# Fetching the down weights of one FFN pair ahead of the next pair's gate and up products

## The chip, the cores and the metric

The kernel runs on one core of one Trainium2 chip. The metric is the time of one execution on the device, in microseconds (us); lower is better. TensorE (PE in the profile) does the matrix products, VectorE (DVE) and ScalarE (ACT) the elementwise work, GpSimd (POOL) some subtractions, and SyncE (SP) issues every DMA of this kernel from a single queue.

## The reference

One layer on a sequence of 2048 tokens with 1024 features. After an RMS norm the input is projected; stick-breaking attention (4 heads), chunked softmax attention with a relative bias (8 heads) and a short gated convolution run side by side; their normalised outputs go through one output projection and are added to the input. Then comes the feed-forward network (FFN), with 2816 hidden features:

```python
def stick_breaking_attention(q, k, v):      # 4 heads of 64
    for o in range(n):                      # key block i - o for query block i, 128 x 128
        z = jnp.einsum('bhnqd,bhnkd->bhnqk', qb[:, :, o:], kb[:, :, :n - o])
        log_rest = jax.nn.log_sigmoid(-z)   # masked on the diagonal
        after = jnp.einsum('bhnqj,js->bhnqs', log_rest, after_mat) + carry[:, :, o:, :, None]
        w = jnp.exp(jax.nn.log_sigmoid(z) + after)
        out = out.at[:, :, o:].add(jnp.einsum('bhnqk,bhnkd->bhnqd', w, vb[:, :, :n - o]))
        carry = carry.at[:, :, o:].add(jnp.sum(log_rest, axis=-1))

def swiglu(x, w_gate, w_up, w_down):
    return (jax.nn.silu(x @ w_gate) * (x @ w_up)) @ w_down

        x = x + y @ w_out[l]
        x = x + swiglu(rmsnorm(x, ffn_norm_w[l]), w_gate[l], w_up[l], w_down[l])
```

## The kernel before

**Two halves, woven.** The 2048 tokens are worked on in two halves of two groups of 512 tokens. `weave()` writes TensorE's program: it alternates pieces of attention with steps of a generator `fill()`, which holds the projections and then, for the first half's two groups, the output projection and the FFN (`ffn_group`). So the FFN of the first half runs beside the attention of the second half. TensorE's order is fixed by the order in which the code is written. The other engines and the SP queue are put in order by a scheduler, and each then runs its own list in order: an instruction that waits holds everything behind it on that engine.

**An attention piece** of the stick-breaking heads computes scores on TensorE (L583 to L586, into one of three `sc` buffers), two sigmoids on ScalarE (L605 and L606, which read the `sc` buffer and so free it), a running product over the keys on VectorE (the scan at L609), a product (L614), transposes on TensorE (L548), their copy to 16 bits (L550 on ScalarE, L551 on VectorE), and the product with the values (L561, L566).

**The FFN of a group.** The 2816 hidden columns are cut into 22 blocks of 128. `gated(f)` makes one block: 24 products for the gate and 24 for the up projection (L318 to L320; each 32-bit operand is held as two 16-bit parts), then tanh and products (L851 to L854), and its high and low parts `gh` (L856) and `gl` (L857). Blocks go in pairs. The product with the down weights of a pair, `down(prev)`, comes after the first block of the next pair: for each of 8 tiles of the output, 6 products into an `sc` buffer (L868 high weight, L869 low weight, L870 high weight with `gl`) and an addition to the row on VectorE (L871). `down` is called for a "set" of two blocks of weights, eleven times a group.

**The weights.** `load_down(f)` brings one block of down weights: a DMA of 512 KB into a raw buffer `wr` (L254), a cast to the high part `wh` on ScalarE (L256), and a subtraction for the low part `wl` on GpSimd (L258). The gate and up weights come through `Weights`: `load` fetches two raw blocks (L179) and sums their squares on ScalarE (L181) to find a scale, and `split` scales and casts them on ScalarE (L223, L224), subtracts on GpSimd (L225) and stores the parts to DRAM (L229). This is done while the first group runs; the second group reloads the parts. `get(f)`, at the start of `gated(f)`, also calls `split` for block f+1 and `load` for block f+2. All raw weights, of the gate, up and down projections, share **one ring of four `wr` buffers**: a load must wait until the buffer's last reader, a GpSimd subtraction (L225 or L258), is done. All split parts share a ring of eight.

Of the kernel before, what the change touches and what calls it, by code (L numbers as in the profile page):

```python
# [34 lines left out]
def f32(ap):  # L35
    return ap.bitcast(F32)
# [3 lines left out]
def trunk(ctx: ExitStack, tc: tile.TileContext, x, anw, w_in, qnw, knw, biasx, conv_w, onw, w_out,  # L40
          fnw, w_gate, w_up, w_down, out):

    nc = tc.nc
# [44 lines left out]
    def sc1():  # L88
        return ps.tile([128, 512], F32, name="sc", tag="sc", bufs=3)
# [161 lines left out]
    def load_down(f, low):  # L251

        raw = wp.tile([128, D], F32, name="wr", tag="wr", bufs=4)
        nc.sync.dma_start(raw, w_down[f * 128:(f + 1) * 128, :])  # L254
        hi = wp.tile([128, D], F32R, name="wh", tag="w16")
        nc.scalar.copy(hi, raw)  # L256
        lo = wp.tile([128, D], F32R, name="wl", tag="w16")
        low.tensor_tensor(lo, raw, f32(hi), ALU.subtract)  # L258
        return hi, lo
# [462 lines left out]
    def y_norms(half):  # L722
        assert traced[half], half
        groups = HALVES[half]
        gain = gain_row("o")
        for i, g in enumerate(groups):
            for t in range(4):
                later(6.0 * (4 * i + t), lambda T=g * 4 + t: y_norm(T, gain))
# [47 lines left out]
    def fill():  # L776

        H = [{}, {}, {}]
        W = stream
        rows = [x_rows(H[0], HALVES[0]), x_rows(H[1], HALVES[1]), y_rows(H[2], HALVES[0])]  # L780
        for half, groups in enumerate(HALVES):
            if half == 0:
                yield from rows[0].ahead()
                rows[0].patient = True
            yield from v_block(H[half], groups, W, C_VA, 0, rows[half])
            if half == 0:
                late_consts()
            yield from stick_qk(H[half], groups, W, 0)
            later(8.0, lambda half=half: done.add((half, 0)))
            yield from stick_qk(H[half], groups, W, 1)  # L790
            later(8.0, lambda half=half: done.add((half, 1)))
            yield from conv_block(H[half], groups, W, 0)
            for p in range(4):
                if half == 1 and p == 3:
                    y_norms(0)
                if p % 2 == 0:
                    yield from v_block(H[half], groups, W, C_VB + 128 * p, 4 + 2 * p)
                yield from chunk_qk(H[half], groups, W, p)
                later(20.0, lambda p=p, half=half: done.add((half, 2 + p)))
            yield from conv_block(H[half], groups, W, 1, rows[half + 1].ahead)  # L800
        yield from out_proj(H[2], HALVES[0], W, rows[2], frows[0])
        for g in HALVES[0]:
            yield from ffn_group(g, frows[0], g == HALVES[0][-1])
# [9 lines left out]
    def paired(f):  # L813

        if f not in PAIRED:
            ds = DS["gu", f][0]
            e = consts.tile([128, 2], F32, name=f"gu{f}")
            nc.vector.tensor_scalar(e[:, 0:1], ds[:, 0:1], 0.5, None, op0=ALU.mult)
            nc.vector.tensor_tensor(e[:, 1:2], e[:, 0:1], ds[:, 1:2], ALU.mult)
            PAIRED[f] = e  # L820
        return PAIRED[f]

    def hidden(u, h):

        (wh, wl), (hh, hl) = u, h
        o = acc()
        yield from mm3(o, lambda k: wh[:, k, :], lambda k: wl[:, k, :], lambda k: hh[:, k, :],
                       lambda k: hl[:, k, :], KT)
        return o

    def ffn_group(g, rows, last):

        yield from rows.need(g, 2)
        h = rows.H[g]
        X1 = []
        with tc.issue_after(last_row[0].ins):
            for t in range(4):
                x1 = xp.tile([128, D], F32, name="x1", tag="xt")
                nc.sync.dma_start(x1, x1d[g * 4 + t])
                X1.append(x1)  # L840

        def part(name):
            return ap.tile([128, 520], F32R, name=name, tag="w2")[:, :GRP]

        def gated(f):

            u = stream.get(("gu", f))
            e = paired(f)
            o = yield from hidden(u[0], h)
            sg = ap.tile([128, 520], F32, name="sg", tag="w2")[:, :GRP]  # L850
            nc.scalar.activation(sg, o, AF.Tanh, scale=e[:, 0:1])  # L851
            nc.vector.scalar_tensor_tensor(sg, sg, 1.0, o, op0=ALU.add, op1=ALU.mult)  # L852
            o = yield from hidden(u[1], h)
            nc.vector.scalar_tensor_tensor(sg, sg, e[:, 1:2], o, op0=ALU.mult, op1=ALU.mult)  # L854
            gh, gl = part("gh"), part("gl")
            nc.scalar.copy(gh, sg)  # L856
            nc.vector.tensor_tensor(gl, sg, f32(gh), ALU.subtract)  # L857
            return gh, gl

        def down(G, W):  # L860
            n = len(G)
            for t in range(4):
                cs = slice(t * 128, (t + 1) * 128)
                for c in range(2):
                    cc = slice(c * 512, (c + 1) * 512)
                    o = sc1()
                    for i, ((gh, gl), (wh, wl)) in enumerate(zip(G, W)):
                        nc.tensor.matmul(o, gh[:, cs], wh[:, cc], start=i == 0, stop=False)  # L868
                        nc.tensor.matmul(o, gh[:, cs], wl[:, cc], start=False, stop=False)  # L869
                        nc.tensor.matmul(o, gl[:, cs], wh[:, cc], start=False, stop=i == n - 1)  # L870
                    nc.vector.tensor_tensor(X1[t][:, cc], o, X1[t][:, cc], ALU.add)  # L871
                    yield 0.65 * n

        prev = None
        for i in range(0, NF, 2):
            G = []
            for f in range(i, min(i + 2, NF)):
                G.append((yield from gated(f)))
                if prev is not None:
                    yield from down(prev[0], [load_down(e, nc.gpsimd) for e in prev[1]])  # L880
                    prev = None
            prev = (G, range(i, i + len(G)))
            if i in (8, 14):
                if last:
                    if i == 14:
                        y_norms(1)
                else:
                    yield from rows.ahead()
        yield from down(prev[0], [load_down(e, nc.gpsimd) for e in prev[1]])
        for t in range(4):  # L890
            T = g * 4 + t
            nc.sync.dma_start(out[T * 128:(T + 1) * 128, :], X1[t])
# [197 lines left out]
```

## Time and profile before

| | |
|---|---|
| time, median of 3 runs | 2824.76 us (2823.86 to 2832.62) |
| profiled execution | 2830.86 us, of it 2829.0 us from first to last instruction |
| mean granted TensorE clock | 0.958 of full speed |
| busy: TensorE, VectorE, ScalarE, GpSimd | 2590.3, 1567.4, 1067.8, 465.3 us |
| TensorE's share of the span | 92% |
| `wr` loads of down weights (L254) | 66 of 512 KB, median 4.1 us from issue to landing |

The profile is of one execution. The engines run side by side, so their busy times don't add up to the span. The idle time of an engine is put down to the instruction or DMA that ended last before it went on ("x waited for y"). Idle time matters where the engine is the one that the others wait for.

### The profile page before, as it was taken

What the parts mean: (1) busy time and instruction counts of PE and PEld (TensorE: products, weight loads), DVE (VectorE), ACT (ScalarE), POOL (GpSimd) and SP (SyncE); (2) the same over time, 40 slices, a digit from 0 to 9 for tenths busy, and PEclk for the clock granted to TensorE, in tenths of its full rate; (3) what the DMA queues carried; (4) which work ended last, traced back from release to release, by engine and by line L of the source; (5) the groups of instructions that cost most, each with busy time, mean ns of one, the idle gap of its engine ahead of it and who ended that gap; (6) DMA issues with size and microseconds to landing.
All of it is one profiled execution on the core that took longest, in us unless ns stands there. A gap on an engine that the chain in (4) does not pass through costs nothing. (4 is left out here: it accounts for less than half of the span.)

```text
span 2829.0 us, 41973 instructions
## 1 busy us (share of the span) xinstructions
PE 2590.3 (92%) x16258; PEld 1742.9 (62%) x16258; DVE 1567.4 (55%) x3601; ACT 1067.8 (38%) x2016; POOL 465.3 (16%) x433
## 2 busy tenths in 40 slices
PE   5998899999879888887889999997999999999999
PEld 4476667688557645554556666653774555665556
DVE  5456876556986665666666666645333223333224
ACT  5465555444444554554554444421112111111110
POOL 1123310022321122223222111123000000000000
PEclk8999999999989988998899999998999999999999
DMA  7544465454348543243336444234563111111101
GB/s 240 181 154 138 124 200 155 145 149 154 127 166 259 162 124 110 93 129 127 105 117 203 144 133 139 92 133 165 197 195 122 53 45 60 45 45 61 51 23 60
DMA packets 254567, 362.42 MB, mean 128 GB/s; under 512 B 78240, under 2 KB 169376, under 8 KB 254368
## 3 DMA queue, kind: packets, MB, share of 16 engines
q1 hardware_dynamic: 254368, 359.75, 39.8%
q8 instruction: 127, 2.08, 0.3%
q14 instruction: 72, 0.59, 0.1%
HBM read 254.81 MB, written 104.86 MB: 127 GB/s over the span
## 5 line engine op out<-in xcount | busy, mean ns | idle before, releaser
L318 PE MATMUL acc<-hh,w 128*128 128x512 f16 x1728 | 661.4, 383 | 13.8 <-DVE sg L852 11.0
L319 PE MATMUL acc<-hl,w 128*128 128x512 f16 x1728 | 658.8, 381 | 0.0
L320 PE MATMUL acc<-hh,w 128*128 128x512 f16 x1728 | 658.4, 381 | 0.0
L318 PE MATMUL acc<-w,hh 128*128 128x256 f16 x1408 | 393.8, 280 | 4.0 <-ACT w L224 4.0
L319 PE MATMUL acc<-w,hh 128*128 128x256 f16 x1408 | 392.3, 279 | 1.8 <-POOL w L225 1.8
L320 PE MATMUL acc<-w,hl 128*128 128x256 f16 x1408 | 392.2, 279 | 0.1
L320 PEld LDWEIGHTS <-w 128*128 128x128 f16 x1728 | 170.0, 98 | 207.0 <-issue 5.9
L318 PEld LDWEIGHTS <-w 128*128 128x128 f16 x1728 | 169.9, 98 | 178.8 <-issue 21.5
L319 PEld LDWEIGHTS <-w 128*128 128x128 f16 x1728 | 170.3, 99 | 166.4 <-issue 17.5
L551 DVE SCALAR_TENSOR_TENSOR wtl<-tp,wth 128x512 f16<-128x512 f32 (+3 forms) x384 | 197.3, 533 | 133.4 <-ACT wth L550 133.2
L609 DVE TENSOR_TENSOR_SCAN re<-re,zero 128x512 f32<-128x512 f32 (+3 forms) x160 | 221.7, 1386 | 73.2 <-ACT re L606 72.7
L225 POOL TENSOR_TENSOR w<-wr,w 128x1024 f16<-128x1024 f32 x76 | 165.6, 2199 | 452.8 <-ACT w L224 283.9
L997 DVE SCALAR_TENSOR_TENSOR sg<-acc,ds,sg 128x512 f32<-128x512 f32 x44 | 33.0, 751 | 346.8 <-PE acc L320 346.8
L868 PE MATMUL sc<-wh,gh 128*128 128x512 f32 x352 | 161.2, 458 | 60.8 <-ACT wh L256 50.7
L550 ACT ACTIVATE wth<-tp 128x512 f16<-128x512 f32 (+3 forms) x384 | 171.8, 471 | 96.0 <-PE tp L548 92.7
L574 POOL TENSOR_TENSOR yu<-yu 128x64 f32<-128x64 f32 x192 | 75.0, 391 | 723.1 <-ACT yu L573 696.6
L1019 DVE TENSOR_TENSOR x<-sc,x 128x512 f32<-128x512 f32 x176 | 121.6, 692 | 109.6 <-PE sc L1017 109.0
L869 PE MATMUL sc<-wl,gh 128*128 128x512 f32 x352 | 151.2, 429 | 25.5 <-POOL wl L258 25.5
L871 DVE TENSOR_TENSOR x<-sc,x 128x512 f32<-128x512 f32 x176 | 120.6, 688 | 92.4 <-PE sc L870 90.0
L652 ACT ACTIVATE s<-s,nm 128x640 f32<-128x640 f32 (+4 forms) x128 | 97.4, 761 | 182.0 <-DVE nm L650 181.7
L583 PE MATMUL sc<-k,q 128*128 128x320 f32 (+3 forms) x384 | 164.6, 433 | 1.3 <-DVE hl L276 1.3
L256 ACT CAST wh<-wr 128x1024 fp32r<-128x1024 f32 x66 | 68.6, 1042 | 246.4 <-PE sc L1016 180.1
(168 smaller groups left out, 4614.7 us busy)
## 6 DMA issues: line engine op xcount, KB each, us to landing
w<-wd SPq DMA_DIRECT2D x136, 512.0 KB, 4.1
wd<-w SPq DMA_DIRECT2D x76, 512.0 KB, 2.7
wr<-in_w_down SPq DMA_DIRECT2D x66, 512.0 KB, 4.1
q<-qd SPq DMA_DIRECT2D x192, 128.0 KB, 2.9
k<-kd SPq DMA_DIRECT2D x56, 256.0 KB, 3.9
wr<-in_w_gate SPq DMA_DIRECT2D x22, 512.0 KB, 4.2
wr<-in_w_up SPq DMA_DIRECT2D x22, 512.0 KB, 5.7
xt<-in_x SPq DMA_DIRECT2D x16, 512.0 KB, 5.0
```

Of the source, the lines that this page charges most:

```text
L225: nc.gpsimd.tensor_tensor(w[:, 1, :], raw, w[:, 0, :], ALU.subtract)
L318: nc.tensor.matmul(o, sh(k), mh(k), start=(k == 0), stop=False)
L319: nc.tensor.matmul(o, sh(k), ml(k), start=False, stop=False)
L320: nc.tensor.matmul(o, sl(k), mh(k), start=False, stop=(k == n - 1))
L550: nc.scalar.activation(wh[:, s], tp[:, c], AF.Copy, scale=WSC)
L551: nc.vector.scalar_tensor_tensor(wl[:, s], tp[:, c], WSC, wh[:, s], op0=ALU.mult, op1=ALU.subtract)
L583: nc.tensor.matmul(z[:, :n + lead], q1[:, cols], kc, start=True, stop=False)
L609: nc.vector.tensor_tensor_scan(re[:, :N], re[:, :N], zero.to_broadcast([128, N]), start, ALU.mult, ALU.add)
L868: nc.tensor.matmul(o, gh[:, cs], wh[:, cc], start=i == 0, stop=False)
L869: nc.tensor.matmul(o, gh[:, cs], wl[:, cc], start=False, stop=False)
L871: nc.vector.tensor_tensor(X1[t][:, cc], o, X1[t][:, cc], ALU.add)
L1019: nc.vector.tensor_tensor(x1, o, x1, ALU.add)
```

## The change

In the loop of `ffn_group` the down weights of the previous pair are asked for before `gated(f)` of the next pair's first block is written, and no longer after it. The call of `down` itself, with its products, stays where it was. The last set of a group, whose call stands behind the loop, is as before; ten of eleven sets a group are moved. Nothing is computed in another way, and no ring changes its size.

```diff
             for f in range(i, min(i + 2, NF)):
+                W = [] if prev is None else [load_down(e, nc.gpsimd) for e in prev[1]]
                 G.append((yield from gated(f)))
                 if prev is not None:
-                    yield from down(prev[0], [load_down(e, nc.gpsimd) for e in prev[1]])
+                    yield from down(prev[0], W)
                     prev = None
```

What this does to the order of the engines is shown around the second set of the first group, whose products stand right behind the last L320 at about 1056 us of the trace. The first rows are of the SP queue before; `wr` are raw weights, `wd` the stored split parts, `q` and `k` are attention operands, and the bracket holds the engines and queues that the row waits for:

```order
L179 DMA wr_13660<-in_w_up 128x8x128
L697 DMA q1_14324<-qd1_10_176 64x512 [waits DMAHW3_49,PE_49]
L697 DMA q2_14325<-qd1_10_176 64x512 [waits DMAHW4_49,PE_49]
L697 DMA q1_14324<-qd1_11_177 64x512 [waits DMAHW5_49]
L697 DMA q2_14325<-qd1_11_177 64x512 [waits DMAHW6_49]
L678 DMA k_15415<-kd1_10_152 64x1024 [waits DMAHW7_49]
L680 DMA k_15415<-kd1_00_150 64x1024 [waits DMAHW0_49]
L678 DMA k_15415<-kd1_11_153 64x1024 [waits DMAHW1_49]
L229 DMA wd22_0_13651<-w16_13643 128x2048 [waits DMAHW2_49,Pool_49]
L229 DMA wd22_1_13652<-w16_13647 128x2048 [waits DMAHW3_49,Pool_49]
L254 DMA wr_13779<-in_w_down 128x1024 [waits DMAHW4_49]
L254 DMA wr_13785<-in_w_down 128x1024 [waits DMAHW5_49]
```

And the SP queue after, from about the same place in the program (the two `wd22` stores are the same ones, seen from both sides):

```order
L254 DMA wr_13633<-in_w_down 128x1024 [waits DMAHW0_49]
L575 DMA ydr1_99<-yu_13578 128x64 [waits DMAHW1_49,Pool_49]
L254 DMA wr_13639<-in_w_down 128x1024 [waits DMAHW2_49]
L697 DMA q1_14324<-qd1_10_176 64x512 [waits DMAHW3_49,PE_49]
L697 DMA q2_14325<-qd1_10_176 64x512 [waits DMAHW4_49,PE_49]
L697 DMA q1_14324<-qd1_11_177 64x512 [waits DMAHW5_49]
L179 DMA wr_13668<-in_w_gate 128x8x128 [waits DMAHW6_49,DMAHW0_49,Pool_49]
L179 DMA wr_13672<-in_w_up 128x8x128 [waits DMAHW7_49,DMAHW2_49,Pool_49]
L697 DMA q2_14325<-qd1_11_177 64x512
L678 DMA k_15415<-kd1_10_152 64x1024 [waits DMAHW1_49]
L229 DMA wd22_0_13663<-w16_13655 128x2048 [waits Pool_49]
L229 DMA wd22_1_13664<-w16_13659 128x2048 [waits DMAHW3_49,Pool_49]
```

The two loads of down weights stood behind the stores of the next block's split parts, and now stand ahead of the `q` loads. The loads of raw gate and up weights (L179) that stood at their place now come later, and each waits for GpSimd, and by the rings for the subtraction of the down weights whose buffer it takes.

The rows of ScalarE before, at the time just ahead of the same set, from the sigmoids of one attention piece (`be_13677`) to those of the piece two further on:

```order
L605 ACTIVATE be_13677<-sc_13674 128x512 [waits PE_49]
L606 ACTIVATE re_13678<-sc_13674 128x512
L550 ACTIVATE wth_13690<-tp_13692 128x512 [waits PE_49]
L851 ACTIVATE sg_13719<-acc_13667,gu4_13664 128x512 [waits PE_49]
L605 ACTIVATE be_13732<-sc_13729 128x128 [waits PE_49]
L606 ACTIVATE re_13733<-sc_13729 128x128 [waits DVE_49]
L550 ACTIVATE wth_13748<-tp_13750 128x512 [waits PE_49]
L256 CAST wh_13781<-wr_13779 128x1024 [waits DMAHW7_49,DMAHW4_49]
L256 CAST wh_13787<-wr_13785 128x1024 [waits DMAHW7_49,DMAHW5_49]
L856 CAST gh_13775<-sg_13719 128x512 [waits DVE_49]
L605 ACTIVATE be_13803<-sc_13799 128x512 [waits PE_49]
L606 ACTIVATE re_13804<-sc_13799 128x512
```

And after, from the same place:

```order
L181 ACTIVATE junk_13670,ws_13667<-wr_13668 128x1024 [waits DMAHW6_49]
L605 ACTIVATE be_13689<-sc_13686 128x512 [waits PE_49]
L181 ACTIVATE junk_13674,ws_13667<-wr_13672 128x1024 [waits DMAHW7_49,Activation_49]
L606 ACTIVATE re_13690<-sc_13686 128x512
L550 ACTIVATE wth_13702<-tp_13704 128x512 [waits PE_49]
L851 ACTIVATE sg_13731<-acc_13679,gu4_13676 128x512 [waits PE_49]
L605 ACTIVATE be_13744<-sc_13741 128x128 [waits PE_49]
L606 ACTIVATE re_13745<-sc_13741 128x128 [waits DVE_49]
L550 ACTIVATE wth_13760<-tp_13762 128x512 [waits PE_49]
L181 ACTIVATE junk_13936,ws_13933<-wr_13934 128x1024 [waits DMAHW4_49,Activation_49]
L181 ACTIVATE junk_13940,ws_13933<-wr_13938 128x1024 [waits DMAHW5_49,Activation_49]
L856 CAST gh_13787<-sg_13731 128x512 [waits DVE_49]
```

The two casts of down weights (L256) are gone from the stretch: they now stand 8 and 6 rows ahead of its first row. Four L181, which read raw gate and up weights and wait for their DMAs, have come into it. Two had stood at the casts' new places and now stand around the sigmoids of the first piece; the other two had stood behind the last row shown.

TensorE's own rows keep their order, but not their waits. Before, around the first score product that stands behind the set's first tile:

```order
L583 MATMUL sc_13799<-k_13539,q1_13547 128x512
L585 LDWEIGHTS identb_82
L585 MATMUL sc_13799<-never_87,identb_82 128x128
L586 MATMUL sc_13799<-k_13539,q2_13548 128x512
L868 MATMUL sc_13809<-wh_13781,gh_13301 128x512 [waits PE_49]
```

And after:

```order
L583 MATMUL sc_13799<-k_13539,q1_13547 128x512 [waits Activation_49]
L585 LDWEIGHTS identb_82
L585 MATMUL sc_13799<-never_87,identb_82 128x128
L586 MATMUL sc_13799<-k_13539,q2_13548 128x512
L868 MATMUL sc_13809<-wh_13635,gh_13313 128x512 [waits PE_49,Activation_49]
```

The score product L583 and the next tile's first L868 take `sc` buffers that two earlier sigmoids free (the L606 that write `re_13690` and `re_13745`), and both now wait for ScalarE themselves. Before, the wait of the set's first product for the later cast L256 had covered these two.

## Rows read from the trace of the kernel before

**Rows 1.** The page: busy time and share of TensorE.
```profile
PE 2590.3 (92%) x16258; PEld 1742.9 (62%) x16258; DVE 1567.4 (55%) x3601; ACT 1067.8 (38%) x2016; POOL 465.3 (16%) x433
```
**Rows 2.** Waits of TensorE, 1003 to 1500 us: total, times, longest.
```profile
PE sc L868 <- ACT wh L256: 50.7, 9, 6.8
PE sc L869 <- POOL wl L258: 25.5, 18, 2.0
PE sc L273 <- DVE hl L276: 7.4, 2, 4.8
```
**Rows 3.** Stretches: busy time of PE, PEld, DVE, ACT, POOL; then granted clock.
```profile
1003.10:1499.90 496.80, 409.52 (x2218) 253.96 (x2218) 321.10 (x577) 261.30 (x432) 138.63 (x75) 0.88 0.37 117
1593.30:1859.80 266.50, 264.27 (x1723) 177.78 (x1722) 159.56 (x470) 111.87 (x257) 45.30 (x67) 1.00 0.40 122
1018.80:1056.40 37.60, 37.56 (x229) 22.98 (x228) 25.04 (x44) 22.76 (x37) 8.99 (x5) 1.00 0.37 104
```
**Rows 4.** Nine stretches behind the waits of rows 2, PE alone: first and sum.
```profile
1005.10:1018.80 13.70, 7.33 (x19) 0.50 0.44 146
...
sum 106.00, PE 61.42; mean PE 6.82
```
**Rows 5.** Timeline around the second set: start, duration, instruction [idle before it].
```profile
1054.37 3.23 DVE L609 TENSOR_TENSOR_SCAN re<-re,zero 128x512 f32<-128x512 f32 x1
...
1057.63 0.28 ACT L606 ACTIVATE re<-sc 128x128 f32<-128x128 f32 x1 [2.31 <-DVE re L609]
...
1061.86 1.04 ACT L256 CAST wh<-wr 128x1024 fp32r<-128x1024 f32 x1 [3.47 <-DMA wr<-in_w_down]
...
1062.96 0.80 PE L868 MATMUL sc<-wh,gh 128*128 128x512 f32 x1 [6.59 <-ACT wh L256]
1063.04 4.66 POOL L258 TENSOR_TENSOR wl<-wr,wh 128x1024 fp32r<-128x1024 f32 x2 [6.52 <-ACT wh L256]
...
1065.44 0.79 PE L869 MATMUL sc<-wl,gh 128*128 128x512 f32 x1 [1.69 <-POOL wl L258]
...
1065.71 2.54 DVE L857 TENSOR_TENSOR gl<-sg,gh 128x512 fp32r<-128x512 f32 x1 [4.29 <-ACT gh L856]
```
**Rows 6.** Timeline of the SP queue ahead of the second set.
```profile
1038.85 0.43 SPq L179 DMA_DIRECT2D wr<-in_w_gate  x1
1039.68 0.66 SPq L575 DMA_DIRECT2D ydr<-yu  x1
1040.38 0.47 SPq L179 DMA_DIRECT2D wr<-in_w_up  x1
...
1054.46 2.41 SPq L229 DMA_DIRECT2D wd<-w  x2
1056.92 0.42 SPq L254 DMA_DIRECT2D wr<-in_w_down  x1
```
**Rows 7.** DMA issues from 1003 to 1500 us: count, KB, median us to landing.
```profile
wr<-in_w_down SPq DMA_DIRECT2D x19, 512.0 KB, 5.0
...
wr<-in_w_up SPq DMA_DIRECT2D x17, 512.0 KB, 4.5
```
**Rows 8.** Waits of TensorE in the second group, 1500 to 1980 us.
```profile
PE sc L868 <- DVE x L871: 9.1, 18, 3.9
```
**Rows 9.** Waits of ScalarE, 1003 to 1500 us.
```profile
ACT junk L181 <- DMA wr<-in_w_gate: 41.1, 11, 4.8
...
ACT junk L181 <- DMA wr<-in_w_up: 4.5, 5, 2.0
```
**Rows 10.** Timeline of ScalarE: one load's sum of squares.
```profile
1047.48 1.06 ACT L181 ACTIVATE junk<-wr 128x1024 bf16<-128x1024 f32 x1 [2.00 <-DMA wr<-in_w_up]
```
**Rows 11.** Timeline of VectorE: a scan with no GpSimd work beside it.
```profile
1021.12 1.22 DVE L609 TENSOR_TENSOR_SCAN re<-re,zero 128x512 f32<-128x512 f32 x1
```
**Rows 12.** Groups of instructions, 1003 to 1500 us: busy us, mean ns of one.
```profile
L258 POOL TENSOR_TENSOR wl<-wr,wh 128x1024 fp32r<-128x1024 f32 x20 | 50.7, 2552 | 49.9 <-ACT wh L256 49.9
...
L606 ACT ACTIVATE re<-sc 128x512 f32<-128x512 f32 x48 | 28.4, 592 | 11.4 <-DVE re L609 11.4
```
**Rows 13.** Two stretches with a loaded VectorE, columns as in rows 3.
```profile
720.00:760.00 40.00, 30.64 (x234) 22.72 (x232) 38.95 (x89) 14.85 (x29) 19.39 (x13) 0.91 0.35 120
...
1340.00:1360.00 20.00, 20.00 (x115) 14.35 (x115) 17.25 (x48) 11.45 (x19) 0.32 (x1) 0.92 0.22 61
```

## The prediction, made before the changed kernel was run

> **What bounds the kernel now.** The page comes first: TensorE is busy for 92% of the span, and no other engine comes near it [rows 1]. What can be gained is therefore idle time of TensorE, and time in which it runs at less than its full clock. The second view is the list of its waits, taken for the stretch from 1003 to 1500 us, in which the first group's FFN runs beside attention. Two rows hold nearly all of it: 50.7 us before L868, nine times, for the cast of the high part of the down weights, and 25.5 us before L869, for GpSimd's low part [rows 2]. Together that is 76.2 us at nine sets of down products, and these are the weights that the change asks for earlier. In the second group the same product waits for the addition L871 instead, 9.1 us in 18 waits [rows 8]; its sets don't wait for weights, so there the change has nothing to take away.
>
> The third view shows the stretch itself, and the reader should compare three of its rows. From 1003.1 to 1499.9 us the granted clock was 0.88; in a run of products without a wait inside it, and in the second group's stretch, it was 1.00 [rows 3]. Cut around the waits, the loss has a place: in nine stretches right behind them the granted clock was 0.50, the 1.2 GHz level, and they hold 61.42 us of TensorE's work [rows 4]. At the 2.4 GHz level this work takes half, so the half clock costs a further 30.7 us. For each microsecond of waiting, another 30.7 / 76.2 = 0.40 us was lost behind it.
>
> The timeline of the second set says why the weights are late. The queue issued the two stores of the next block's split parts at 1054.46, for which GpSimd had to be done, and only then, at 1056.92, the first load of down weights [rows 6]. The cast began at 1061.86, after the DMA; TensorE went on at 1062.96 after 6.59 us, and waited 1.69 us more for the low part at 1065.44 [rows 5]. It had been out of work from 1062.96 - 6.59 = 1056.37.
>
> **The change, part by part.** The two loads L254 take the places in the queue that the raw gate and up loads had: 1038.85 and 1040.38 [rows 6], some 17 us ahead of 1056.92. With the median 5.0 us to landing [rows 7] the second lands at about 1045.4. A cast of 1.04 us and two subtractions of 4.66 us together [rows 5] make the last low part ready at 1045.4 + 1.04 + 4.66 = 1051.1, at the latest of these reckonings, where TensorE comes for it at 1056.4. That is 5 us to spare, so **all 76.2 us of waiting for weights go**, and the 30.7 us of half clock with them: 106.9 us. From the profiled execution's 2830.86 us this leaves 2724.0.
>
> What is added: no instruction. The same DMAs, casts and subtractions run, each once, and TensorE's order is the same. The moved sets of the second group were early already and are costed at nothing: their cover is the time for which their weights lie ready, and without it they would wait as the first group's sets do, some 8 us a set.
>
> What is late next are the raw gate and up loads of the block after next. There are four raw buffers; the two L179 now wait for the subtractions of the down weights that just took the buffers, up to 1051.1 by the reckoning above, and the queue stands still behind them: `q` and `k` loads and the next stores. With 4.5 us to landing for the up weights [rows 7] the second lands at about 1056. On ScalarE its L181, of 1.06 us [rows 10], stands ahead of the sigmoid L606 that frees an `sc` buffer, and two products of TensorE beside the set wait for such buffers. So ScalarE is held by a DMA at a place where TensorE soon needs it. The split of that block itself is wanted only one block later, some 18 us, and is covered.
>
> What this returns no row of before shows directly. Bounds: below, the second group's wait, 9.1 / 18 = 0.5 us a set, which stays even where the weights are early [rows 8]; above, 4.8 us, the longest wait of ScalarE's L181 for its load [rows 9] and also the longest of TensorE in this stretch that is not for down weights [rows 2]. I take the mean wait of an L181 for its load, (41.1 + 4.5) / (11 + 5) = 2.85 us [rows 9], because it is this wait that is moved to where TensorE feels it, once a set. Nine sets give 25.7 us, and as each microsecond has cost 0.40 more through the clock, 36 us. By the bounds it is 6 to 60 us.
>
> **The sum:** 2830.86 - 106.9 + 36 = 2760 us against the profiled execution. That one lies 6.1 us above the median 2824.76, so in terms of the median the forecast is 2824.76 - 70.9 = **2754 us**.
>
> One more thing moves: GpSimd's subtractions of down weights. Before, they ran while TensorE stood still, beside L857; now they run beside the scans of attention. A scan took 1.22 us with GpSimd silent [rows 11] and 3.23 us beside a subtraction; L857 took 2.54 us beside one [rows 5]. Two subtractions a set, each lengthening one scan by 2.0 us, make 36 us on VectorE in nine sets. It was busy for 321.1 of 496.8 us [rows 3]; 357 us in a stretch shortened to about 426 us are 84%. In a stretch where it was busy for 86% TensorE had no idle time, in one at 97% it was down to 77% [rows 13]. I cost this at nothing, and the price without that cover is a rival's. The Trainium skill, page "SBUF — State Buffer", section "Who interferes with whom", says that a VectorE instruction with two SBUF inputs contends with a GpSimd instruction that reads SBUF, through a port pair that one of the two holds at a time. The trace agrees in the two pairs of instructions above, 3.23 against 1.22 us; taken at its harshest, with a scan held for the whole of a subtraction, 2.55 us by the trace, VectorE would get 46 us instead of 36, and the sum would stay as it is.
>
> **The rivals.** *All of it is kept.* The `sc` buffers are freed in time and only the second group's half microsecond stays: 106.9 - 6 = 101 us less, so 2724 us; with no return at all 2718. For it: between waits TensorE had no idle time, 37.56 of 37.60 us [rows 3], though ScalarE waited for loads then too. Against it: the two products now wait for ScalarE by name.
>
> *VectorE becomes the limit in part.* The lengthened scans hold back the products that follow them. If TensorE is busy 90% of the stretch, as lies between the two rows of [rows 13], its work at the full clock, 409.5 - 30.7 = 378.8 us, takes 421 us in place of 496.8: 76 us less, 2749 us. The total would be near my forecast for another reason; the waits tell them apart (L548 for VectorE's products, and not L583 or L868 for L606). It is the rule named above that speaks for it.
>
> *Slower.* One mechanism: the chain from the down weights' landing to the sigmoid, each link at its longest. Second load landed 5.0 us after 1040.38, cast 1.04, subtractions 4.66, the raw load longer than its median by the longest time that ScalarE waited for one, 4.5 + 4.8, then L181 1.06, L606 0.59 [rows 12], a scan of 3.23 us and, behind it, the next piece's L606 of 0.59 us, which waits for the scan as its like does in [rows 5]: 1065.85, which is 9.5 us after TensorE's 1056.37. Nine times 9.5 with 0.40 for the clock make 120 us, 13 more than was gained: 2838 us. It decides from 106.9 / (9 x 1.4) = 8.5 us a set on. Against it: it takes every link at its worst in every set.
>
> *Nothing changes.* If the moved L254 had to wait for a raw buffer as long as before, the weights would come at the old time, 2825 us. Against it: the L179 that stood at that place in the queue were issued at 1038.85 and 1040.38 into the same ring.
>
> **How the numbers follow.** The forecast (a part returned, 0.5 to 4.8 us a set, 2724 to 2778) has 0.58; all kept (2714 to 2724) 0.17; VectorE in part 0.10; most returned, up to 8 us a set (2778 to 2818), 0.06; slower 0.05; no change 0.04. The range 2714 to 2795 leaves out the last two and half of the one before them, with a little for ends that I have mis-sized. Less than about 0.3% (8.5 us) a measurement of this kernel can't tell from no change. Faster by more: 0.90 (the upper edge of the fourth case lies within); within: 0.05; slower: 0.05.
>
> **What would show it.** In the trace after, the waits of L868 for the cast and of L869 for the low part should be gone from 1003 to 1500 us, L254 should stand some 17 us ahead of its set, and the granted clock of the stretch should be above 0.95. New waits of TensorE should stand at L583 or L868, for ScalarE's L606, and L181 should wait for its loads at least as long as before. Second-group sets should be as they were. The prediction is wrong if the new waits are over 5 us a set, if the clock stays low without a wait, or if L869 still waits for GpSimd because its subtractions are queued behind L225.

## The result and the profile after

The changed kernel takes 2780.74 us (median of 4 runs, 2779.96 to 2787.71), the kernel before, on the same chip, 2828.69 us (2823.86 to 2833.22). The ratio is 0.9836, with a 95% interval from 0.981 to 0.9863: 1.6% faster, about 46 us on 2825. The forecast was 2754 us, 71 us less; the time lies inside the range given and well short of the forecast.

The page after, first and fifth part. The last row is the group that held the 50.7 us of waiting for the cast; over the whole span the wait is now put down mostly to the addition L871:

```profile
span 2778.2 us, 42004 instructions
...
PE 2567.4 (92%) x16258; PEld 1726.6 (62%) x16258; DVE 1566.9 (56%) x3601; ACT 1064.6 (38%) x2016; POOL 462.3 (17%) x433
...
L868 PE MATMUL sc<-wh,gh 128*128 128x512 f32 x352 | 155.1, 441 | 35.0 <-DVE x L871 22.2
```

The stretch of the first group's nine sets, cut at the same instructions as in [rows 3]: from TensorE's stop before the first set to the start of the tenth (busy time of PE, PEld, DVE, ACT, POOL, then granted clock):

```profile
1001.50:1452.10 450.60, 395.69 (x2219) 244.75 (x2218) 318.94 (x579) 260.97 (x439) 134.53 (x75) 0.95 0.42 131
```

It was 496.80 us with 409.52 us of TensorE in it, and the clock was 0.88. So 46.2 of the 50.8 us by which the span is shorter are here. They split in two: idle time went from 87.3 to 54.9 us, 32.4 less, and TensorE's own busy time from 409.5 to 395.7, 13.8 less, which is the clock. The largest waits of TensorE in the same stretch (total, times, longest):

```profile
PE sc L868 <- DVE x L871: 12.5, 8, 3.8
PE tp L548 <- DVE wtl L551: 10.1, 2, 6.5
PE sc L868 <- ACT re L606: 9.4, 5, 4.3
PE sc L273 <- DVE hl L276: 8.7, 2, 6.4
PE av L561 <- ACT yu L573: 3.5, 2, 2.9
PE sc L273 <- ACT re L606: 3.0, 1, 3.0
```

Against [rows 2], the 76.2 us of waiting for down weights are gone to the last one. In their place stand waits that were small or not there before, 43.8 us in all (54.9 less the 87.3 - 76.2 = 11.1 that were there). Some 14 us of the new ones name ScalarE and 30 us VectorE. A name tells only which engine released TensorE last; what had held that engine up has to be read from the timeline.

The second set shows where one of them comes from. First the SP queue ahead of it, which answers to [rows 6]:

```profile
1031.92 0.43 SPq L254 DMA_DIRECT2D wr<-in_w_down  x1
...
1033.22 0.47 SPq L254 DMA_DIRECT2D wr<-in_w_down  x1
...
1040.77 0.39 SPq L179 DMA_DIRECT2D wr<-in_w_gate  x1
1043.26 0.39 SPq L179 DMA_DIRECT2D wr<-in_w_up  x1
```

The set begins at 1049.1, so the down weights are issued 17 and 16 us ahead; their last subtraction, of a pair that took 4.84 us from 1038.39, was over by 1043.2, 5.9 us early. The raw gate and up loads have to wait for the buffers that these subtractions give back. The timeline of the set itself:

```profile
1049.52 1.02 SPq L179 DMA_DIRECT2D wr<-in_w_up  x1
...
1058.82 1.06 ACT L181 ACTIVATE junk<-wr 128x1024 bf16<-128x1024 f32 x1 [3.30 <-DMA wr<-in_w_up]
...
1059.88 0.60 ACT L856 CAST gh<-sg 128x512 fp32r<-128x512 f32 x1
1060.38 0.59 ACT L605 ACTIVATE be<-sc 128x512 f32<-128x512 f32 x1
1060.87 0.59 ACT L606 ACTIVATE re<-sc 128x512 f32<-128x512 f32 x1
...
1061.51 0.79 PE L868 MATMUL sc<-wh,gh 128*128 128x512 f32 x1 [4.31 <-ACT re L606]
```

Read it from the bottom: TensorE stood 4.31 us for an `sc` buffer that a sigmoid frees; the sigmoid stood behind the copy L856, and that behind the sum of squares L181, which waited 3.30 us for its load, issued at 1049.52. It is the mechanism of the forecast, at 4.3 us instead of the 2.85 taken.

The longest new wait, 6.48 us in the tenth cycle (the one that ends with the tenth set), is of another make:

```profile
1431.48 5.12 POOL L258 TENSOR_TENSOR wl<-wr,wh 128x1024 fp32r<-128x1024 f32 x2 [6.54 <-ACT wh L256]
...
1434.32 2.30 DVE L214 TENSOR_SCALAR wsc<-wsc 128x2 int32<-128x2 int32 x1
...
1436.72 2.19 ACT L223 ACTIVATE wr<-wr,wsc 128x1024 f32<-128x1024 f32 x2 [2.75 <-DVE wsc L214]
...
1438.81 1.98 ACT L224 CAST w<-wr 128x1024 f16<-128x1024 f32 x2
...
1440.69 0.75 ACT L550 ACTIVATE wth<-tp 128x384 f16<-128x384 f32 x2
1441.20 0.89 DVE L551 SCALAR_TENSOR_TENSOR wtl<-tp,wth 128x384 f16<-128x384 f32 x2 [2.66 <-ACT wth L550]
...
1441.91 1.30 PE L548 MATMUL tp<-ident,s 128*128 128x128 f32 x5 [6.48 <-DVE wtl L551]
```

Beside the two subtractions of down weights an operation on 128x2 elements (L214) holds VectorE for 2.30 us; the scaling and casts of the next block (L223, L224) wait for it on ScalarE, and the copy L550 that TensorE needs stands behind those. The wait is put down to VectorE, but against L214's median of 0.17 us the hold is some 2.1 of the 6.48 us; the scalings and casts ahead of the copy, 2.19 and 1.98 us, are ScalarE's own work.

### The profile page after: what moved, and what is told of

Its sections match the earlier page's. It is cut to its first block, busy times and chain, and to the rows that moved or that the text cites. A ratio compares the mean times of both kernels' runs of the same rounds, so it can differ in the third digit from the quotient of the medians.

```text
span 2778.2 us, 42004 instructions
## 1 busy us (share of the span) xinstructions
PE 2567.4 (92%) x16258; PEld 1726.6 (62%) x16258; DVE 1566.9 (56%) x3601; ACT 1064.6 (38%) x2016; POOL 462.3 (17%) x433
## 5 line engine op out<-in xcount | busy, mean ns | idle before, releaser
L318 PE MATMUL acc<-hh,w 128*128 128x512 f16 x1728 | 662.7, 384 | 16.3 <-DVE sg L852 16.1
L320 PE MATMUL acc<-hh,w 128*128 128x512 f16 x1728 | 659.7, 382 | 0.0
L320 PE MATMUL acc<-w,hl 128*128 128x256 f16 x1408 | 390.5, 277 | 1.3 <-DVE rry L102 1.3
L320 PEld LDWEIGHTS <-w 128*128 128x128 f16 x1728 | 170.4, 99 | 208.1 <-issue 7.5
L551 DVE SCALAR_TENSOR_TENSOR wtl<-tp,wth 128x512 f16<-128x512 f32 (+3 forms) x384 | 197.5, 533 | 133.0 <-ACT wth L550 132.7
L609 DVE TENSOR_TENSOR_SCAN re<-re,zero 128x512 f32<-128x512 f32 (+3 forms) x160 | 209.8, 1311 | 68.7 <-ACT re L606 68.2
L550 ACT ACTIVATE wth<-tp 128x512 f16<-128x512 f32 (+3 forms) x384 | 171.8, 471 | 92.6 <-PE tp L548 89.4
L868 PE MATMUL sc<-wh,gh 128*128 128x512 f32 x352 | 155.1, 441 | 35.0 <-DVE x L871 22.2
L1020 DVE TENSOR_TENSOR x<-sc,x 128x512 f32<-128x512 f32 x176 | 121.7, 692 | 109.6 <-PE sc L1018 109.0
L583 PE MATMUL sc<-k,q 128*128 128x320 f32 (+3 forms) x384 | 164.6, 433 | 3.6 <-DVE x L871 1.8
L256 ACT CAST wh<-wr 128x1024 fp32r<-128x1024 f32 x66 | 68.0, 1044 | 239.6 <-PE sc L1017 180.1
L318 PEld LDWEIGHTS <-hh 128*128 128x128 f16 x1408 | 140.1, 99 | 29.1 <-issue 8.0
L320 PEld LDWEIGHTS <-hl 128*128 128x128 f16 x1408 | 140.2, 100 | 22.1 <-issue 2.1
```

Of the source, the lines that this page charges most:

```text
L318: nc.tensor.matmul(o, sh(k), mh(k), start=(k == 0), stop=False)
L320: nc.tensor.matmul(o, sl(k), mh(k), start=False, stop=(k == n - 1))
L550: nc.scalar.activation(wh[:, s], tp[:, c], AF.Copy, scale=WSC)
L551: nc.vector.scalar_tensor_tensor(wl[:, s], tp[:, c], WSC, wh[:, s], op0=ALU.mult, op1=ALU.subtract)
L583: nc.tensor.matmul(z[:, :n + lead], q1[:, cols], kc, start=True, stop=False)
L609: nc.vector.tensor_tensor_scan(re[:, :N], re[:, :N], zero.to_broadcast([128, N]), start, ALU.mult, ALU.add)
```

## The experiments

Two theories are tried. **A**: what came back is ScalarE, which runs its list in order and stands at instructions that wait for raw weights. **B**: it is VectorE, lengthened by GpSimd's subtractions that now run beside attention. Each ratio is against the kernel before on the same chip. In the table, the stretch is the first group's, cut as above; its length, TensorE's busy time and the clock are from the view of stretches of each profile, and idle is the difference of the first two.

| kernel | ratio to before, 95% interval | stretch | busy | idle | clock |
|---|---|---|---|---|---|
| before | | 496.8 | 409.5 | 87.3 | 0.88 |
| the change | 0.9836 (0.981 to 0.9863) | 450.6 | 395.7 | 54.9 | 0.95 |
| e1, five raw buffers | 0.9778 (0.9764 to 0.9793) | 440.4 | 394.1 | 46.3 | 0.95 |
| e2, old place, five buffers | 0.9854 (0.9839 to 0.9869) | 462.2 | 399.5 | 62.7 | 0.92 |
| e3, no sums of squares | 0.9787 (0.9767 to 0.9806) | 439.0 | 393.0 | 46.0 | 0.95 |
| e4, short subtraction | 0.9748 (0.973 to 0.9767) | 431.0 | 388.3 | 42.7 | 0.97 |
| e5, scan's zeros in PSUM | 1.0011 (1.0 to 1.0021) | 466.5 | 395.8 | 70.7 | 0.93 |
| e6, e3 and e4 together | 0.9659 (0.9632 to 0.9686) | 412.4 | 385.9 | 26.5 | 0.97 |
| e7, load early, cast late | 0.975 (0.9729 to 0.9771) | 423.8 | 387.9 | 35.9 | 0.98 |
| e8, e5 with five buffers | 0.9915 (0.989 to 0.994) | 445.2 | 390.5 | 54.7 | 0.95 |
| e9, e7 with five buffers | 0.9748 (0.9724 to 0.9772) | 439.3 | 396.1 | 43.2 | 0.95 |
| e10, e7, subtraction on VectorE | 0.9731 (0.9712 to 0.975) | 419.8 | 386.6 | 33.2 | 0.98 |
| e11, one of two early | 0.9899 (0.9878 to 0.9919) | 476.8 | 403.5 | 73.3 | 0.91 |
| e12, the change, subtraction on VectorE | 0.9751 (0.9726 to 0.9777) | 436.6 | 392.1 | 44.5 | 0.95 |

**e1: a fifth raw buffer.**

```diff
-        raw = wp.tile([128, D], F32, name="wr", tag="wr", bufs=4)
+        raw = wp.tile([128, D], F32, name="wr", tag="wr", bufs=5)
```

(and the same in `Weights.load`).

> The change with five raw buffers instead of four. After the change TensorE still waits 54 us between 1001 and 1470 us, some 43 of it in places where it did not wait before. Theory A: these waits come from ScalarE, which runs its list in order and stands still at casts and sums of squares that wait for raw weight DMAs (66 us in 1000 to 1460 us), because four buffers make the loads come late. Then a fifth buffer lets loads start earlier, ScalarE's waits for raw loads fall from 66 to about 40 us, TensorE's waits from 54 to about 35, and the time is 65 to 75 us below before instead of the change's 46 to 51. Theory B: VectorE is the limit, lengthened by GpSimd's subtractions beside it; then a buffer changes nothing and the time stays 44 to 54 us below before.

The time came out between the two, 62 us below before: more than B allows, short of A's 65 to 75, and not for A's reason alone. Of the gain over the change, 6.6 us lie ahead of the stretch (it begins at 994.9 instead of 1001.5) and 10 us in it. ScalarE's waits for raw weights fell only from 66 to 57 us, not to 40, and TensorE's idle time to 46, not 35.

**e2: the kernel before with five buffers.**

> The kernel before with five raw buffers; the down weights are asked for at the old place. It tells whether the late weights were a matter of the place in the queue or of the ring. If of the place (theory A and the prediction): the loads are still behind the stores of the split parts, the waits at L868 and L869 stay above 50 of 76 us, and the time is 0 to 25 us below before. If the ring alone had held the weights back: the waits at L868 and L869 fall below 25 us and the time is 40 to 60 us below before, as with the change. Theory B says nothing here beyond the same.

TensorE's waits of this kernel in the stretch:

```profile
PE sc L869 <- POOL wl L258: 29.2, 16, 3.1
PE sc L868 <- ACT wh L256: 20.5, 9, 4.6
```

49.7 of 76.2 us are left, so at the old place the weights are still late; yet the time is 42 us below before, 11 us of it ahead of the stretch. Neither branch of the expectation held whole: the lateness had been made by the place in the queue and by the ring, each in part.

**e3: no sums of squares for the FFN.**

```diff
-                with nc.allow_low_precision(reason="a bound, to a factor of two"):
-                    nc.scalar.activation(junk(), raw, AF.Square, accum_out=ss[:, i:i + 1])
+                if key[0] != "gu":
+                    with nc.allow_low_precision(reason="a bound, to a factor of two"):
+                        nc.scalar.activation(junk(), raw, AF.Square, accum_out=ss[:, i:i + 1])
                 tiles.append(raw)
+            if key[0] == "gu":
+                nc.vector.memset(ss, 1.0)
```

> The change, and the sums of squares of the FFN's raw gate and up blocks are left out: a constant stands for them, from which the same kind of scale is made. ScalarE then has some 36 us less work in the first group and no longer stands at these loads when they land, only at the scaling one block later. Theory A: TensorE's waits for the sigmoid L606 (9.4 us) and for the tanh and copy chain behind it vanish, its waits in the stretch fall from 54 to about 30 us, and the time is 70 to 85 us below before. Theory B: VectorE's work is the same, so the waits for L871 and L551 stay and the time is 46 to 56 us below before.

As A says, the waits at L868 and L583 for a sigmoid are gone (9.8 us before this edit), and the stretch is 11.6 us shorter. The waits that name VectorE stayed (16.0 us for L871, 11.0 us for L551), as B says. The time lies between the two, 60 us below before. This run takes away the sums themselves as well as the waits for their loads (ScalarE is busy for 220.6 us in the stretch instead of 261.0), so it doesn't tell standing at a load from the work done there.

**e4: GpSimd's subtraction all but left out.**

```diff
-        low.tensor_tensor(lo, raw, f32(hi), ALU.subtract)
+        if low is nc.gpsimd:
+            nc.gpsimd.memset(f32(lo)[:, 8:], 0.0)
+            low.tensor_tensor(lo[:, :8], raw[:, :8], f32(hi)[:, :8], ALU.subtract)
+        else:
+            low.tensor_tensor(lo, raw, f32(hi), ALU.subtract)
```

> The change, and in the attention's FFN the low part of the down weights is left out but for 8 of 1024 columns: GpSimd fills the rest with zeros, so that it reads almost nothing from SBUF, and the order of waits is kept. Theory B: without these subtractions the scans and additions of VectorE beside them get back to their short durations (a scan of 3.2 us to 1.2), some 36 us of VectorE's time in nine sets, TensorE's waits for L871 and L551 (23 us) fall to under 10, and the time is 65 to 80 us below before. Theory A: ScalarE still stands at the loads, TensorE's waits fall by under 10 us in all, and the time is 46 to 58 us below before.

The stretch (columns as above):

```profile
1003.10:1434.10 431.00, 388.32 (x2218) 241.47 (x2217) 292.45 (x578) 256.56 (x431) 107.90 (x91) 0.97 0.44 136
```

VectorE has 26.5 us less to do than in the change (318.94), with the same instructions, and the stretch is 19.6 us shorter. B's mechanism is there; its size is 26 us where the prediction reckoned with 36. The waits for L871 and L551 went from 22.6 to 14.5 us, not under 10. GpSimd itself has 26.6 us less as well, so this run alone doesn't separate a lengthened VectorE from a GpSimd that is free earlier. Earlier loads are not the reason: ScalarE's waits for raw weights are as long as after the change, 66.8 us against 66.2.

It is not the scans that got shorter. Groups of instructions from 1000 to 1460 us (busy us, mean ns of one), first after the change and then here, where L613 is the old L609 and L616 the old L612:

```profile
L609 DVE TENSOR_TENSOR_SCAN re<-re,zero 128x512 f32<-128x512 f32 x49 | 74.2, 1515 | 21.7 <-ACT re L606 21.5
L613 DVE TENSOR_TENSOR_SCAN re<-re,zero 128x512 f32<-128x512 f32 x49 | 74.0, 1511 | 25.5 <-ACT re L610 25.2
L612 DVE TENSOR_TENSOR be<-be,re 128x1 f32<-128x1 f32 x45 | 22.8, 506 | 38.0 <-ACT be L605 37.7
L616 DVE TENSOR_TENSOR be<-be,re 128x1 f32<-128x1 f32 x45 | 17.9, 398 | 42.1 <-ACT be L609 42.0
```

The moved subtractions had held up shorter operations: L612, by 4.9 us in all, L857 by 5.7 and L214 by 4.2. Nor was VectorE busier after the change than before it, 318.9 against 321.1 us [rows 3]: it was lengthened before as well, at other instructions. No run leaves the subtractions out of the kernel before.

**e5: the scan's zeros in PSUM.** The zeros get the last column of the bank that holds the `av` product.

```diff
-    zero = consts.tile([128, 1], F32, name="zero")
+    avz = ps.tile([128, 512], F32, name="av", tag="av", bufs=1)
+    zero = avz[:, 511:512]
     nc.vector.memset(zero, 0.0)
...
-        return ps.tile([128, 2 * HD], F32, name="av", tag="av", bufs=1)
+        return avz[:, :2 * HD]
```

> The change, and the scan L609 takes its row of zeros from PSUM instead of SBUF, so that one of its two inputs is no longer in SBUF; every value is the same. In the first group after the change the 62 scans take 14.5 us longer in all than at their short durations, and the waits of TensorE put down to VectorE are 39.5 us. Theory B in the form of a shared read port: scans beside GpSimd's subtractions keep 1.2 to 1.3 us, the 14.5 us shrink below 4, TensorE's waits for VectorE fall to about 28 us, and the time is 55 to 65 us below before. If what lengthens a scan is not its second SBUF input, its long durations stay at 3 us and the time stays 44 to 52 us below before.

First the scans in the first group after the change, then in this kernel (shortest, median and longest in ns), and then TensorE's largest wait here:

```profile
L609 DVE TENSOR_TENSOR_SCAN re<-re,zero x62: 472/1275/3232, 1003.9 to 1413.8; 128x512 f32<-128x512 f32 x49, 128x384 f32<-128x384 f32 x5, 128x128 f32<-128x128 f32 x4, 128x256 f32<-128x256 f32 x4
```

```profile
L610 DVE TENSOR_TENSOR_SCAN re<-re,av x62: 469/1222/1283, 1000.7 to 1445.3; 128x512 f32<-128x512 f32 x48, 128x256 f32<-128x256 f32 x5, 128x384 f32<-128x384 f32 x5, 128x128 f32<-128x128 f32 x4
```

```profile
PE av L562 <- DVE re L610: 51.2, 15, 9.4
```

No scan takes longer than 1.28 us any more, where the longest took 3.23, though 16 scans of the stretch still run beside a subtraction of GpSimd: the second SBUF input is what had made a scan long. The Trainium skill, page "SBUF — State Buffer", section "Who interferes with whom", says that a VectorE instruction with two SBUF inputs contends with a GpSimd instruction that reads SBUF. The trace agrees, in the two rows of scans above. The time is that of the kernel before, some 50 us more than the change's: the zeros now share a tile with `av`, and TensorE waits 51.2 us for scans before it may write there. 32 us of it were lost ahead of the stretch, which begins at 1033.4. What the scans' lengthening costs the kernel can't be read from this run. **e8** repeats it with five buffers:

> The change with the zeros of the scan in PSUM and with five raw buffers. Five buffers alone were at a ratio of 0.978, 62 us below before. If the scan's contention is real and apart from the loads: 70 to 80 us below before. If the zeros in PSUM do nothing: 58 to 66 us below.

It was 27 us below before, short of both figures, with the same wait on top (40.4 us), and adds nothing.

**e6: e3 and e4 together.**

> The change without the sums of squares of the FFN's gate and up blocks (a constant stands for them) and with the low part of the down weights left out but for 8 columns, together. Apart, the first took the first group from 450.7 to 439.0 us and the second to 431.0. If ScalarE's standing at loads (theory A) and GpSimd's subtractions beside VectorE (theory B) cause different waits, the two gains add: group one at about 419 us, the time 80 to 92 us below before, little of TensorE's wait for L606 or VectorE left but some 20 us. If they are one chain, the second brings nothing on top: 428 to 432 us, the time 68 to 75 us below before.

They add, and a little more: the stretch is 38.2 us shorter than the change's, against 11.6 + 19.6 = 31.2 apart, and the time 98 us below before. The waits follow: those that name ScalarE are 3.6 us, against 16.3 after the change, and those that name VectorE 22.7 against 38.3. The two causes are two, and together they are worth 38 of the 61 us that had come back.

**e7: the load early, the cast and subtraction at the old place.**

```diff
+    def raw_down(f):
+        raw = wp.tile([128, D], F32, name="wr", tag="wr", bufs=4)
+        nc.sync.dma_start(raw, w_down[f * 128:(f + 1) * 128, :])
+        return raw
...
-                W = [] if prev is None else [load_down(e, nc.gpsimd) for e in prev[1]]
+                R = [] if prev is None else [raw_down(e) for e in prev[1]]
                 G.append((yield from gated(f)))
                 if prev is not None:
-                    yield from down(prev[0], W)
+                    yield from down(prev[0], [load_down(e, nc.gpsimd, r) for e, r in zip(prev[1], R)])
```

> The change cut in two: the DMA of the down weights stays at the early place, the cast and the subtraction are asked for at the old place, after the next block's products. Theory A: ScalarE no longer stands at the casts for the DMA (32 us), but the raw buffers are held longer, so the gate and up loads come later and L181 waits more; TensorE's waits for L606 are at least the 9.4 us of the change, and the waits for the cast and the low part are some 5 to 15 us of the 76: 30 to 48 us below before. If it is the DMA alone that had to be early, nothing comes back and the time is 50 to 60 us below before.

It beats the change by 23 us, more than either branch allowed. TensorE's waits in the stretch (L873 and L874 are the old L868 and L869, L611 the old L606):

```profile
PE sc L874 <- POOL wl L263: 13.3, 12, 1.8
PE sc L873 <- DVE x L876: 11.3, 11, 1.7
PE sc L278 <- DVE hl L281: 5.8, 2, 3.1
PE sc L873 <- ACT re L611: 2.5, 2, 2.1
```

and ScalarE's waits for loads:

```profile
ACT junk L181 <- DMA wr<-in_w_gate: 31.5, 12, 4.9
ACT junk L181 <- DMA wr<-in_w_up: 3.1, 5, 0.7
```

13.3 us of waiting for the low part come back, as expected. But ScalarE stands 35 us at loads instead of 66, since the cast no longer does, and TensorE waits 2.5 us for a sigmoid instead of 12.8. The expectation that the gate and up loads would hold ScalarE the more was wrong. VectorE is no less busy than after the change (324.6 against 318.9 us). But the subtraction has moved too, and TensorE's waits that name VectorE fell from 38.3 to 19.7 us; so this run alone doesn't say how much of the gain is A's. e10 and e12 say more.

**e9: e7 with five buffers.**

> The early load with the cast and subtraction at the old place, and five raw buffers. With four it was at a ratio of 0.975, the change with five at 0.978. If a raw load that comes late is what still holds ScalarE (theory A; 35 us of waits of L181 for loads), the fifth buffer takes 8 to 15 us off: 80 to 90 us below before. If the loads no longer reach TensorE, the buffer brings only what it brings ahead of the FFN, some 7 us: 75 to 80 us below before.

The same time as e7. The stretch begins 9 us earlier (993.5 against 1002.6) and is 15.5 us longer in the profiled execution, which was 7 us above this kernel's median; waits for the low part rise from 13.3 to 24.7 us. The buffer doesn't add to the late cast.

**e10 and e12: the subtraction on VectorE**, in e7 and in the change: `nc.vector` in place of `nc.gpsimd` in the loop's call of `load_down`.

> The early load with the cast at the old place, four raw buffers, and the subtraction of the moved down weights on VectorE instead of GpSimd. A subtraction of 2.65 us on GpSimd becomes one of some 1.3 us on VectorE; TensorE's 13.3 us of waits for the low part should shrink, and the scans beside the subtractions be short again. Theory B: the 20 subtractions add 26 us to VectorE and take 15 to 20 us of lengthening away, so VectorE comes out even; TensorE's waits fall by some 5 to 10 us: 75 to 90 us below before. If VectorE's own work is the limit: waits for L871 rise above 20 us and the time is 55 to 70 us below before.

> The change with the subtraction of the moved down weights on VectorE instead of GpSimd, the values as before. Leaving the subtractions out brought the first group from 450.7 to 431.0 us. Theory B (they cost by sharing a port with VectorE): VectorE gets 26 us of work and loses some 15 of lengthening, the waits for VectorE stay within 5 us of the change's, and the time is 42 to 58 us below before. If VectorE's own share of the time is what counts: 30 to 42 us below before.

The stretch of e12 (columns as above):

```profile
1007.60:1444.20 436.60, 392.13 (x2220) 244.78 (x2218) 303.97 (x593) 260.01 (x436) 90.56 (x57) 0.95 0.44 135
```

VectorE takes on 19 subtractions of 1.22 us, 23.2 us, and is yet busy for 303.97 us where it was 318.94 in the change. So about 38 us of lengthening are gone, and the stretch is 14 us shorter: B, this time with every value computed. It brought 70 us below before, more than was expected. Yet the waits of TensorE that name VectorE hardly fell, from 38.3 to 36.0 us; those for a sigmoid did, from 12.8 to 4.7. What VectorE loses reaches TensorE in part through ScalarE, which waits for it. In e10 VectorE comes out even (320.8 against 324.6 us) and the gain over e7 lies within the intervals; it is the fastest of the kernels that leave nothing out, at 2753.61 us, but not told apart from e7, e9 and e12. Over the change, the late cast and subtraction alone brought some 24 us (e7), the subtraction on VectorE alone 22 (e12), and both 29 (e10). So the two moves overlap: once the subtraction is off GpSimd, casting late brings only some 7 us more, within the intervals, and a good part of e7's gain may be B's.

**e11: only the first block of a pair early.**

```diff
-                W = [] if prev is None else [load_down(e, nc.gpsimd) for e in prev[1]]
+                W = [] if prev is None else [load_down(prev[1][0], nc.gpsimd)]
                 G.append((yield from gated(f)))
                 if prev is not None:
-                    yield from down(prev[0], W)
+                    yield from down(prev[0], W + [load_down(e, nc.gpsimd) for e in prev[1][1:]])
```

> Half the change: only the first block of a pair is loaded, cast and subtracted ahead of the next block; the second at the old place. The wait for the second block's cast and low part comes back: the first tile's fourth product needs it, so by the timeline of the change TensorE stops 1 us later than in the kernel before. If the set waits for its last load: 40 to 60 us of waits for the weights remain and the time is 5 to 25 us below before. If each block carries its share: half the gain, 20 to 28 us below before.

TensorE's waits for the weights in the stretch:

```profile
PE sc L868 <- ACT wh L256: 37.7, 9, 6.5
PE sc L869 <- POOL wl L258: 14.0, 8, 1.9
```

51.7 of 76.2 us are left, so the set does wait for its last load; the stretch is 20 us shorter than before. The whole time is 30 us below before, a little more than either figure; some 9 us of it lie behind the stretch's end and are not explained here.

## Why the prediction was right and where it was off

- **All waiting for weights goes: right.** No wait for L256 or L258 is left in the stretch. The loads moved by the 17 us forecast, and in the second set the last low part was ready 5.9 us early, against 5 reckoned. Two signs came out less well: the clock of the stretch was to be above 0.95 and stands at 0.95 in the view, and L181 was to wait for its loads at least as long as before, but its waits fell from 45.6 to 33.9 us.
- **The clock follows: right.** 76.2 - 32.4 = 43.8 us of waiting came back, and 30.7 - 13.8 = 16.9 us of the half clock with it: 0.39 per microsecond, where 0.40 was taken.
- **What comes back: mis-sized, and this is the term that failed.** "I take the mean wait of an L181 for its load ... 2.85 us ... once a set" gave 25.7 us of new waits, 36 with the clock. Measured were 43.8 and 60.7 us: 4.9 us a set, just above the upper bound that the text had set (4.8). The part that was reckoned came out smaller than reckoned: the new waits that name ScalarE are 14 us, and e3 puts the mechanism at 11.6 us of the stretch, where 36 had been taken. That the time still lies in the range is partly luck, since the size taken was too large for one cause and another was left out. The measured 2780.7 us lies just above the forecast's own case (2724 to 2778, 0.58), in the case that had 0.06.
- **Why it was too small: VectorE was costed at nothing.** The place was "I cost this at nothing", on the ground that VectorE would be busy only 84% of the stretch. It was busy for 318.9 of 450.6 us, 71%, and still 30 of the 43.8 us of new waits name it. The 36 us that it was to gain did not come: it was busy no longer than before, and the scans are as long without the moved subtractions as with them (e4). These hold short operations instead. A mean share is no cover where an instruction held for 2 us stands right ahead of work that TensorE needs next. Leaving the subtractions out gives back 19.6 us of the stretch (e4), moving them 14 us (e12).
- **The rival "VectorE in part" had 0.10 and was part of the truth**, though not by way of the scans. ScalarE held at its loads, the forecast's mechanism, is real too (11.6 us in e3, with the sums' own work in it). The two together are 38 us (e6). Of the other 23 us of the 61 nothing is settled.
- **"All kept", "slower" and "nothing changes" fell.** New waits came, the kernel was faster, and the loads left their old place. On the last, e2 shows that a fifth buffer at the old place would have brought almost as much (ratio 0.9854): the ring was a cause of the lateness beside the queue, which the prediction put down to the queue alone.

## What to carry to other kernels

Fetching earlier means two things, and it pays to try moving them apart: the DMA wants to be early, but the cast that waits for it, on an engine that runs in order, may stand better where its data has landed (e7, with the subtraction moved too: 23 us better than moving all; with the subtraction on VectorE only some 7). When a stall is removed, the work that used to lie inside it, here two subtractions a set on GpSimd, lands beside something else; price it there, instruction by instruction, and not by the mean share of the engine. And where a ring of buffers is shared by two streams, try one more buffer before reordering: here it was worth 42 us, where the change was worth 48. And a wait's name is the last releaser, not the cause: the 6.48 us put down to VectorE were mostly ScalarE's own work.

## What the runs showed of the hardware that was not expected

An operation of VectorE on 128x2 elements (L214, median 0.17 us) took 2.30 us beside GpSimd's subtraction, and L612, on one column, had a median of 0.16 us and a longest of 2.23 us after the change, also beside one: these small operations were held for some 2 us, as long as the scan of 3.23 us that takes 1.22 alone. And the clock did not follow the sum of the waits: in e7, with 35.9 us of waiting and none of it longer than 3.1 us, the granted clock of the stretch was 0.98, against 0.95 with 54.9 us and waits of up to 6.5 us after the change. In e6, with less waiting in all (26.5 us) but one wait of 3.8 us, it was 0.97. Two stretches of the changed kernel, with 6.9 and 7.7 us of idle time, differ likewise (columns as above); the first has its longest wait at 2.9 us, the second has one of 6.4 us:

```profile
1119.60:1168.10 48.50, 41.58 (x244) 25.42 (x243) 33.59 (x71) 29.01 (x49) 14.71 (x8) 1.00 0.35 110
1168.10:1221.80 53.70, 45.96 (x262) 28.61 (x261) 36.20 (x67) 30.77 (x52) 14.66 (x8) 0.94 0.37 119
```
